# Eight plain row tiles instead of six at the head of a Strassen-Winograd matmul, with a new head order and early casting loads

## The chip, the cores and the metric

The kernel runs on one core of one Trainium2 chip. The metric is the device time of one execution in microseconds (us), taken from several executions; their median is what is compared. A profile of one execution is shown beside it.

## The reference

```python
batch, m, k, n = 16, 512, 1024, 768      # x: (16, 512, 1024), w1 and w2: (1024, 768), all float32
y1 = np.matmul(x, w1)
y2 = np.matmul(x, w2)
return (np.tanh(y1) * y2).astype(np.float32)
```

So there are 8192 rows of x, or 64 row tiles of 128 rows. Each goes through two products, with w1 (t = 0) and with w2 (t = 1), and the two results are joined by a tanh and a multiplication.

## The kernel before

**Two kinds of row tiles.** The first HEAD = 6 row tiles are computed plainly in bfloat16. For one tile and one weight there are 8 steps over the inner dimension (k = 0 to 7), each with a matmul of 512 columns ("F", line 265) and one of 256 columns ("G", line 268). The other 58 row tiles go in 29 pairs. A pair is multiplied by one weight with a Strassen-Winograd scheme in float16: seven block products p1 to p7 (line 399), each of four matmuls of 384 columns, instead of eight. One pair with one weight is a *unit*; there are 58 units. The plain tiles need only a cast of w and a transposed x. The units need more: the power-of-two scale of w (the sum of |w|), the blocks b11, b21, b22 and t1 to t4 of w in float16, a scaled float16 copy of x, its transpose, and the block sums s1 to s4 of the transposed x (line 380).

**Who does what.** TensorE multiplies. The plain tiles 0 to 3 are loaded in float32 and transposed on TensorE (`T00` to `T31`, line 216; `T20` is the first half of the columns of tile 2), and evacuated and cast by `e00` to `e31`. Tiles 4 and 5 are loaded by GpSimd DMAs that cast to bfloat16 (`Lx4`, `Lx5`, line 241) and then transposed by DMA transposes on the queue of SP (`e41`, `e51`, line 245). A one-element GpSimd copy (line 240) from the row block of w2 that has to land first holds each of these casting loads back. The x of the pairs is loaded by SP (`Lp00` is pair 0, upper tile; line 332), summed by ScalarE (`ax`, line 338), scaled by VectorE (`rx`), cast (`cx`, line 358, or on ScalarE line 360) and transposed by a DMA transpose on SP (`Tx00`, `Tx01`, line 366). The weights are loaded as 16 row blocks (`La0` to `La7` for w1, `Lb0` to `Lb7` for w2, line 248), cast (`ca`, `cb`) and summed (`absa`, `absb`, line 258). `parta`, `suma` and `scalea` make the scale of w1 out of the sums; `suma` is a matmul with ones (line 298), into the PSUM bank that SCALE_BANK names. The plain results go through `tanh0F` (ScalarE, line 281) and `mul0F` (VectorE, line 285) and are stored by `st0` to `st5` (line 288). In a unit, ScalarE copies PSUM out (`seed` L413, `s5` and `u2` L417) and does the tanh (L430), and VectorE adds (`c12`, `c22`, L422) and multiplies (L436).

**Order.** Each engine works strictly in its order. For the head and the first ten units (PLANNED = 10) the order on every engine is the list ORDER, written out by hand. A planner walks it (`schedule`) with costs and dependencies only to decide in which order the program emits the instructions. `m41F3` in the lists is tile 4, weight w2, F, k = 3; `p5.0` is product 5 of unit 0. SEQUENCE says which pair and weight a unit is. The remaining units are emitted at slots of a fixed pitch, by a formula. At the head of the SP queue stands LOADS, in which x0 to x3 are loaded in halves, between the blocks of w.

**Rings.** The float32 x has 6 buffers, the 16-bit x (`xh`) 4, the transposed x (`xT`) 10, the output (`o`, one buffer for two tiles) 3. Three PSUM pairs serve the units; the head uses the eight banks as they become free.

Of the kernel before, what the change touches and what calls it, by code (L numbers as in the profile page):

```python
# [13 lines left out]
def kernel(  # L14
# [16 lines left out]
    nc = tc.nc  # L31
# [8 lines left out]
    F = 512  # L40
    G = N - F
    HEAD = 6
# [6 lines left out]
    LOADS = ("x0.0 a0 x1.0 a1 x2.0 a2 x0.1 x3.0 a3 x1.1 x2.1 a4 x3.1 a5 a6 a7 b0 b1 b2 b3 b4 b5 b6 b7").split()  # L49
    ABS = ((1, 1, 1, 1, 1, 1, 1, 1), (2, 0, 2, 0, 2, 0, 1, 1))  # L50
    SCALE_BANK = (3, 1)
# [6 lines left out]
        "e01": "dve", "e10": "act", "e11": "dve", "e20": "act", "e21": "dve", "e31": "dve", "ca0": "act",  # L58
        "ca2": "act", "cx31": "act", "cx40": "act", "cx61": "act"
# [3 lines left out]
            T00 T10 T20 m10F0 m00F0 m20G0 m00G0 T01 T30 m20F0 m00F1 m00F2 T11 m30F0 m30F1 m00F3 m10F1 m10F2  # L63
            T21 m10G0 m00G1 m00G2 m20G1 m10F3 m10F4 m20F1 m20F2 m20F3 m20F4 m20F5 T31 m30F2 m20F6 m00F4 m00F5
            m00F6 m00F7 m20F7 m30G0 m30G1 m30G2 m30G3 m30G4 m30G5 m30G6 m30F3 m30F4 m30F5 m30F6 m30F7 m01G0
            m11F0 m11F1 m11G0 m21G0 m31G0 m31G1 m01F0 m01F1 m11G1 m01G1 m21G1 suma m21G2 m11G2 m11F2 m01G2
            m31G2 m01F2 m00G3 m00G4 m20G2 m20G3 m20G4 m20G5 m20G6 m20G7 m30G7 m00G5 m00G6 m00G7 m10G1 m10G2
            m10G3 m10G4 m10G5 m10G6 m10G7 m10F5 m10F6 m10F7 m31G3 m31G4 m11G3 m11G4 m11G5 m01F3 m01F4 m01F5
            m31G5 m11F3 m01G3 m01G4 m01G5 m40F0 m40F1 m40F2 m40F3 m31G6 m01G6 m11G6 m01G7 m31G7 m40F4 m40F5
            m40F6 m40F7 m11F4 m11F5 m21G3 m21G4 m21G5 m21G6 m21G7 m01F6 m01F7 m11F6 m11F7 m21F0 m21F1 m21F2  # L70
            m21F3 m21F4 m21F5 m21F6 m21F7 m40G0 m50G0 m40G1 m50G1 m50G2 m40G2 m40G3 m40G4 m31F0 m31F1 m31F2
            m31F3 m31F4 m31F5 m31F6 m31F7 m11G7 m50F0 m50F1 m50F2 m50F3 m50F4 m50F5 m50F6 sumb m50F7 m41F0
            m41F1 m41F2 m41F3 m41F4 m40G5 m40G6 m40G7 m50G3 m50G4 m50G5 m50G6 m50G7 m41G0 m51G0 m51G1 m51G2
            m51G3 m51G4 m51G5 m51G6 p1.0 m41G1 m41G2 m41G3 m41G4 m41G5 m41G6 m41G7 p5.0 p2.0 p6.0 m51G7 p3.0
            m41F5 m41F6 m41F7 p7.0 p1.1 p1.2 p4.0 p5.1 p2.1 p6.1 p5.2 p3.1 p7.1 p2.2 p6.2 p4.1 p1.3 p3.2 p7.2
            p5.3 p2.3 p6.3 p4.2 p3.3 p7.3 m51F0 m51F1 m51F2 m51F3 m51F4 m51F5 p4.3 p1.4 p1.5 p5.4 p2.4 p6.4
            p5.5 p2.5 p7.4 p3.4 p6.5 p4.4 m51F6 m51F7 p3.5 p7.5 p1.6 p4.5 p5.6 p2.6 p6.6 p1.7 p3.6 p7.6 p5.7
            p2.7 p4.6 p6.7 p1.8 p5.8 p7.7 p3.7 p2.8 p4.7 p6.8 p1.9 p3.8 p7.8 p5.9 p2.9 p4.8 p6.9 p1.10 p3.9
            p7.9 p5.10 p2.10 p4.9
        """,  # L80
        "act": """
            absa0 e10 ca0 e20 absa1 ca2 absa3 absa2 absa4 absa5 absa6 absa7 tanh0F tanh2F absb0 tanh3F absb2
            b21a b22a tanh2G tanh0G tanh1F ax00 tanh4F absb7 ax01 absb4 absb6 ax10 ax11 tanh5F b11b tanh4G
            seed.0 b22b s5.0 f00.0 u2.0 ax21 b21b seed.1 f10.0 seed.2 s5.1 f00.1 u2.1 f11.0 s5.2 ax20 f11.1
            u2.2 f10.1 f01.0 seed.3 ax31 s5.3 u2.3 ax41 f01.1 ax30 ax40 seed.4 seed.5 s5.4 f00.4 u2.4 cx31
            cx40 s5.5 f01.4 u2.5 f10.4 ax51 seed.6 f11.4 s5.6 f00.6 u2.6 seed.7 ax50 f11.6 f01.6 f10.6 u2.7
            seed.8 s5.7 s5.8 ax60 ax61 u2.8 seed.9 f00.8 cx61 s5.9 f10.8 u2.9 f01.8 f11.8 seed.10 s5.10 f00.10
        """,
        "dve": """
            e00 ca1 e01 e30 ca3 e11 ca4 e21 ca5 ca6 ca7 e31 cb1 cb0 parta cb2 cb4 scalea cb5 cb3 cb6 cb7 b11a  # L90
            t1a t2a t4a t3a mul0F mul1F mul2G rx0 cx00 mul2F cx01 mul3F partb mul0G scaleb sx0 rx1 cx10 sx1
            cx11 s3.0 s1.0 s2.0 s4.0 t1b mul4G c12.0 mul4F c22.0 s3.1 s1.1 s2.1 s4.1 t2b t4b t3b c12.1 c22.1
            f00.2 rx2 cx20 cx21 c12.2 f01.2 c22.2 f11.2 f00.3 f10.2 sx2 c22.3 f11.3 c12.3 f10.3 s1.2 s2.2 rx3
            cx30 rx4 s3.2 s4.2 f01.3 c22.4 c12.4 sx3 cx41 mul5F c12.5 c22.5 s1.3 s3.3 s2.3 s4.3 f00.5 f10.5
            f01.5 f11.5 c12.6 c22.6 rx5 cx50 s1.4 s2.4 s3.4 s4.4 cx51 c22.7 c12.7 f00.7 f01.7 f10.7 sx4 rx6
            cx60 c22.8 s1.5 s2.5 s3.5 c12.8 f00.9 sx5 f11.7 c12.9 c22.9 s4.5 f01.9 f10.9 f11.9
        """,
        "dma": """
            Lx0.0 La0 Lx1.0 La1 Lx2.0 La2 Lx0.1 Lx3.0 La3 Lx1.1 Lx2.1 La4 Lx3.1 La5 La6 La7 Lb0 Lb1 Lb2 Lb3
            Lb4 Lb5 Lb6 Lb7 e41 Lp00 e51 Lp01 Lp10 Lp11 Tx00 Lp20 Tx01 st0 Tx10 Lp21 Tx11 Lp30 st4 st2 st1  # L100
            Lp31 st3 Lp40 Lp41 Tx20 Tx21 store1.2 Lp50 store1.3 Tx30 Lp51 Tx31 store0.3 st5 Tx40 Tx41 store0.2
            Lp60 Lp61 Tx50 Tx51 Tx60 Tx61 store0.7 store1.7 store0.9 store0.5 store1.9 store1.5
        """,
        "pool": """
            Lx4 Lx5
# [19 lines left out]
    smpool = pool("sm", 4)  # L125
# [48 lines left out]
    def op(name, engine, cost, due, needs, fn, *args):  # L174
        plan[name] = (engine, cost, [n for n in needs if n], fn, args)
# [61 lines left out]
    def load_cast_head_x(mt):  # L237
        hb[mt] = xhpool.tile([P, K], bf16, tag="xh", name="x_b")

        pin(nc.gpsimd.tensor_copy(hb[mt][:, :1], w_f[1][:, mt - 2, :1]))  # L240
        pin(nc.gpsimd.dma_start(hb[mt], xf[mt]))
# [162 lines left out]

    SEQUENCE = [(0, 0), (1, 0), (0, 1), (1, 1)] + [(i, t) for i in range(2, PAIRS) for t in range(2)]
# [110 lines left out]

    for n, what in enumerate(LOADS):
        i = int(what[1])
        if what[0] == "x":
            op(f"L{what}", "dma", 0.7, n - 200, [], load_head_x, i, int(what[3]))  # L520
        else:
            op(f"L{what}", "dma", 1.0, n - 200, [], load_w, "ab".index(what[0]), i)
    for mt in range(HEAD):
        if mt < 4:
            for h in range(2):
                op(f"T{mt}{h}", "pe", 0.45, 5 + mt + 4 * h, [f"Lx{mt}.{h}", f"e{mt - 1}{h}" if mt else ""], pe_transpose_f, mt, h)
                op2("e", f"e{mt}{h}", ("dve", "act")[h], 4 + mt + 4 * h, [f"T{mt}{h}", f"e{mt}0" if h else "", f"e{mt - 1}0" if mt and not h else ""],
                   evacuate_f, mt, h)
        else:
            op(f"Lx{mt}", "pool", 2.6, 22, [f"Lb{mt - 2}"], load_cast_head_x, mt)  # L530
            op(f"e{mt}1", "dma", 1.3, 20, [f"Lx{mt}", f"e{mt - 1}0" if mt == 4 else f"e{mt - 1}1"], dma_transpose_head, mt)
    for t in range(2):
        for k in range(KO):
            a = "ab"[t]
            op2("c", f"c{a}{k}", "dve", 6 + 1.3 * k + 12 * t, [f"L{a}{k}"], cast_wb, t, k)
            n = ABS[t][k]
            if n:
                op(f"abs{a}{k}", "act", 0.23 + 0.82 * n, 8 + 1.3 * k + 17 * t, [f"L{a}{k + n - 1}"], abs_w, t, k, n)
# [4 lines left out]
    def accumulate(m, t, which, bank, due):  # L543
# [9 lines left out]
        if t == 0:  # L553
            op(out, "act", 0.62, due(KO), last, head_tanh, banks[bank], m, which == "F")
        else:
            op(out, "dve", 0.68, due(KO) + 3, last + [f"tanh{m}{which}"], head_mul, banks[bank], m, which == "F")
# [24 lines left out]
    if HEAD > 4:  # L581
        for n, (mt, t, which, bank) in enumerate(((4, 0, "F", 3), (5, 0, "F", 5), (4, 0, "G", 7), (4, 1, "F", 6), (4, 1, "G", 3),
                                                  (5, 1, "F", 7))):
            accumulate(mt, t, which, bank, lambda k: 29 + 1.7 * n)
        stores(4)
# [17 lines left out]
    ready = lambda i: 43.5 + 0.65 * 7 * min(position[i, 0], position[i, 1]) - 4  # L603
    x_ring = ["e01", "e11", "e21", "e31"]
    for i in range(FIRST + 1):
        due = ready(i)
        for h in range(2):
            n = 2 * i + h
            x_free = "" if n < 2 else x_ring[n - 2] if n < 6 else f"cx{(n - 6) // 2}{n % 2}"
            h_free = f"Tx{(n - 4) // 2}{n % 2}" if n >= 4 else ""  # L610
            op(f"Lp{i}{h}", "dma", 1.35, due - 12, [x_free, f"Lp{(n - 1) // 2}{(n - 1) % 2}" if n else "Lb7"], load_x, HEAD + n)
# [4 lines left out]
            if n >= 10 - HEAD:  # L616
                r = n - 10 + HEAD
                if r < 4:
                    t_need += [f"m{r}1F7", f"m{r - r % 2}1G7", f"m{r - r % 2 + 1}1G7"]
                elif r < HEAD:  # L620
                    t_need += [f"m{r}1F7", "m41G7", "m51G7"]
                else:
                    t_need += of_unit("p4", (r - HEAD) // 2, 1) + of_unit("p3", (r - HEAD) // 2, 1)
# [16 lines left out]
    for u in range(PLANNED + 1):  # L640
        i, t = SEQUENCE[u]
        for name, (engine, cost, z, needs, fn, args) in unit_ops(u).items():
# [19 lines left out]
            op(f"{name}.{u}", engine, cost, 43.5 + 0.65 * (z + 7 * u), [f"{n}.{u}" for n in needs] + more, fn, *args)  # L662
# [64 lines left out]
```

## Time and profile before

| | us |
|---|---|
| median of 7 runs | 324.84 |
| lowest, highest of them | 322.87, 328.54 |
| the profiled execution, its own time | 328.12 |
| span of that execution (first to last instruction) | 326.3 |
| TensorE busy in the span | 310.7 (95%) |
| VectorE, ScalarE busy | 242.2 (74%), 233.2 (71%) |
| granted TensorE clock, mean | 0.977 |

The profiled execution is one of the longest: it is 3.3 us over the median. What lies outside the span is 328.12 less 326.3, 1.8 us. Busy time of TensorE is not time at its peak, since the matmuls overlap; starts of matmuls are what counts. An engine that is busy 74% of the span can still be late in one place, so the stretches of the head are read one by one.

### The profile page before, as it was taken

The page shows a single profiled execution, that of the slowest core. Times are in us where ns is not written, and L with a number is a line of the kernel's source. Part 1 is how long each engine was busy: PE and PEld are TensorE (multiplying, and loading weights), DVE is VectorE, ACT ScalarE, POOL GpSimd, SP SyncE. Part 2 cuts the span into 40 slices and gives each one's busy share as a digit, 9 for nine tenths or more (in the row PEclk, how much of TensorE's full clock was granted, in tenths as well). Part 3 has the DMA queues.
Part 4 walks back from the last instruction along what each step waited for, and adds up shares of the span by engine and source line. Part 5 has one row for each costly group of instructions (what it writes and reads, how often), then busy time and mean ns, then how long its engine had stood idle before and what let it go on. Part 6 is the DMA issues. An engine that isn't in the chain of part 4 may idle for free.

```text
span 326.3 us, 5430 instructions
## 1 busy us (share of the span) xinstructions
PE 310.7 (95%) x1859; PEld 184.6 (57%) x1859; DVE 242.2 (74%) x565; ACT 233.2 (71%) x454; POOL 7.3 (2%) x15
## 2 busy tenths in 40 slices
PE   5998959999999999999999999999999999999994
PEld 2665534655555555555565555555565555555652
DVE  1468636987878777779877777779877777778642
ACT  4685964888877777777777777777777777776551
POOL 1020000000000000000000000000000000000004
PEclk9699996999999999999999999999999999999999
DMA  6998795978999999999899999998899899985322
GB/s 241 394 398 173 242 176 165 333 215 222 313 257 226 317 282 299 237 283 233 249 242 292 263 279 237 255 278 258 252 215 296 262 272 246 270 250 140 121 96 97
DMA packets 84988, 80.58 MB, mean 247 GB/s; under 512 B 65760, under 2 KB 66272, under 8 KB 84960
## 3 DMA queue, kind: packets, MB, share of 16 engines
q1 hardware_dynamic: 84384, 79.32, 88.0%
q0 software_dynamic: 288, 0.52, 0.9%
q10 hardware_dynamic: 288, 0.39, 0.3%
q8 instruction: 14, 0.23, 0.3%
q14 instruction: 14, 0.11, 0.1%
HBM read 39.85 MB, written 25.17 MB: 199 GB/s over the span
## 4 chain that ended last, share of the span: by engine, by line
PE 81%; DMA 13%; DVE 2%; SPq 2%; issue 0%; POOL 0%; ACT 0%; DVEq 0%
PE bank L399 77%; DMA xT<-x_h 5%; DMA x_f<-in_x_dram 4%; PE bank L265 3%; DMA wf<-in_w_dram 2%; DMA x_b<-in_x_dram 2%; DMA xTb<-x_b 1%; SPq L208 1%; PE bank L268 1%; DVE o L436 1%; SPq L248 1%; DVE s L380 1%; DVE c L422 0%; DVE x_h L358 0%; POOL x_b L240 0%
## 5 line engine op out<-in xcount | busy, mean ns | idle before, releaser
L399 PE MATMUL bank<-t,s 128*128 128x384 f16 x696 | 134.0, 328 | 4.7 <-DVE s L380 4.3
L399 PEld LDWEIGHTS <-s 128*128 128x128 f16 x928 | 91.0, 98 | 67.0 <-DVE s L380 4.9
L399 PEld LDWEIGHTS <-xT 128*128 128x128 f16 x696 | 68.2, 98 | 48.1 <-issue 2.7
L399 PE MATMUL bank<-b,xT 128*128 128x384 f16 x464 | 94.7, 328 | 0.6 <-ACT bank L413 0.6
L338 ACT ACTIVATE junk<-x_f 128x1024 bf16<-128x1024 f32 x58 | 60.8, 1049 | 6.9 <-DMA x_f<-in_x_dram 6.8
L422 DVE TENSOR_TENSOR c<-bank,u 128x384 f32<-128x384 f32 x58 | 32.2, 555 | 44.9 <-PE bank L399 42.3
L430 ACT ACTIVATE th<-c,out_r 128x384 f32<-128x384 f32 x58 | 35.1, 610 | 23.4 <-DVE c L422 23.3
L399 PE MATMUL bank<-b,s 128*128 128x384 f16 x232 | 47.9, 330 | 0.0
L399 PE MATMUL bank<-t,xT 128*128 128x384 f16 x232 | 47.1, 325 | 0.1
L417 ACT ACTIVATE u<-bank 128x384 f32<-128x384 f32 x58 | 28.2, 487 | 19.4 <-PE bank L399 18.8
L358 DVE TENSOR_SCALAR x_h<-x_f,pr 128x1024 f16<-128x1024 f32 x55 | 41.0, 747 | 0.3
L430 ACT ACTIVATE th<-bank,out_r 128x384 f32<-128x384 f32 x58 | 33.3, 574 | 7.0 <-PE bank L399 7.0
L436 DVE SCALAR_TENSOR_TENSOR o<-bank,out_r,th 128x384 f32<-128x384 f32 x58 | 35.4, 611 | 1.8 <-PE bank L399 1.6
L413 ACT ACTIVATE bank<-bank 128x384 f32<-128x384 f32 x58 | 28.0, 482 | 10.7 <-DVE o L436 8.1
L417 ACT ACTIVATE s<-bank 128x384 f32<-128x384 f32 x58 | 27.9, 483 | 10.4 <-PE bank L399 7.9
L422 DVE TENSOR_TENSOR c<-bank,s 128x384 f32<-128x384 f32 x58 | 32.1, 553 | 3.4 <-PE bank L399 1.1
L436 DVE SCALAR_TENSOR_TENSOR o<-c,out_r,th 128x384 f32<-128x384 f32 x56 | 33.7, 606 | 0.1
L380 DVE TENSOR_TENSOR s<-xT 128x512 f16<-128x512 f16 x58 | 23.9, 417 | 5.5 <-DMA xT<-x_h 5.5
L265 PE MATMUL bank<-wb,xTb 128*128 128x512 bf16 x96 | 25.4, 394 | 1.3 <-DMA xTb<-x_b 1.3
L258 ACT ACTIVATE junk<-wf 128x768 bf16<-128x768 f32 (+1 forms) x13 | 12.9, 991 | 4.1 <-DMA wf<-in_w_dram 4.0
L265 PEld LDWEIGHTS <-xTb 128*128 128x128 bf16 x96 | 9.7, 103 | 9.6 <-DMA xTb<-x_b 1.6
L268 PE MATMUL bank<-wb,xTb 128*128 128x256 bf16 x96 | 13.9, 277 | 0.0
(48 smaller groups left out, 140.3 us busy)
## 6 DMA issues: line engine op xcount, KB each, us to landing
x_f<-in_x_dram SPq DMA_DIRECT2D x58, 512.0 KB, 5.8
out_dram<-o SPq DMA_DIRECT2D x62, 384.0 KB, 3.4
wf<-in_w_dram SPq DMA_DIRECT2D x16, 384.0 KB, 7.1
x_f<-in_x_dram SPq DMA_DIRECT2D x8, 256.0 KB, 6.5
xT<-x_h SPq DMA_TRANSPOSE x58, 3.7
x_b<-in_x_dram POOLq DMA_DIRECT2D x2, 256.0 KB, 5.3
out_dram<-o ACTq DMA_DIRECT2D x2, 192.0 KB, 2.0
out_dram<-o SPq DMA_DIRECT2D x2, 192.0 KB, 2.3
```

The costliest lines, as they stand in the source:

```text
L258: pin(nc.scalar.activation(junk[:, :n * N].rearrange("p (k n) -> p k n", n=N), w_f[t][:, k:k + n, :], ACT.Abs, accum_out=asum_w[t][:, j:j ...
L265: pin(nc.tensor.matmul(bank, hx[mt][:, k, :], w_b[t][k][:, :F], start=k == 0, stop=k == KO - 1))
L268: pin(nc.tensor.matmul(bank[:, at_:at_ + G], hx[mt][:, k, :], w_b[t][k][:, F:], start=k == 0 and mt % 2 == 0, stop=k == KO - 1, skip_group ...
L338: pin(nc.scalar.activation(junk[:, :K], xs[HEAD + 2 * i + h], ACT.Abs, scale=2.0 ** -12, accum_out=pair_sum[i][:, h:h + 1]))
L358: pin(nc.vector.tensor_scalar(xh, xs.pop(mt), pair_r[i][:, h:h + 1], None, ALU.mult))
L380: pin((nc.vector if eng == "dve" else nc.gpsimd).tensor_tensor(s, st[i, a], st[i, b], op))
L399: pin(nc.tensor.matmul(bank[:, cols], st[i, a][:, k, :], wt[t][b][:, k, cols], start=start and k == 0, stop=stop and k == KH - 1, skip_gro ...
L413: pin(nc.scalar.activation(ub[u]["b"][:, :Q], ub[u]["a"][:, :Q], ACT.Copy))
L417: pin(nc.scalar.activation(c, ub[u][bank][:, :Q], ACT.Copy))
L422: pin(nc.vector.tensor_tensor(c, ub[u][bank][:, :Q], ub[u][other], ALU.add))
L430: pin(nc.scalar.activation(th, v, ACT.Tanh, scale=rs[i][:, 0, h:h + 1]))
L436: pin(nc.vector.scalar_tensor_tensor(o[:, h, q * Q + cols.start:q * Q + cols.stop], v, rs[i][:, 1, h:h + 1], tanhs[i, h, q][:, cols], ALU. ...
```

## The change

HEAD goes from 6 to 8: tiles 6 and 7 become plain, by the casting load and the DMA transpose that tiles 4 and 5 have, and 28 pairs, 56 units, are left. SEQUENCE takes each pair with w1 and then with w2; before, pairs 0 and 1 went with w1 first, and then both with w2. x0 to x3 are loaded whole. The casting loads of tiles 4 to 7 are held back by row blocks 1, 3, 5 and 7 of w2 (before: 2 and 3 for tiles 4 and 5). Both sums of |w| go into bank 5. The second-stage plain tiles alternate between banks 6 and 7. All orders of the head are written out anew, some casts and evacuations change their engine, a pool of small tiles gets 8 buffers, and the planner counts the casting loads and some other DMA work (this only moves where instructions are emitted).

```diff
-    HEAD = 6
+    HEAD = 8
-    LOADS = ("x0.0 a0 x1.0 a1 x2.0 a2 x0.1 x3.0 a3 x1.1 x2.1 a4 x3.1 a5 a6 a7 b0 b1 b2 b3 b4 b5 b6 b7").split()
+    LOADS = ("x0 a0 x1 a1 x2 a2 x3 a3 a4 a5 a6 a7 b0 b1 b2 b3 b4 b5 b6 b7").split()
-    SCALE_BANK = (3, 1)
+    GATE = {4: 1, 5: 3, 6: 5, 7: 7}
+    SCALE_BANK = (5, 5)
     ELSEWHERE = {
-        "e01": "dve", "e10": "act", "e11": "dve", "e20": "act", "e21": "dve", "e31": "dve", "ca0": "act",
-        "ca2": "act", "cx31": "act", "cx40": "act", "cx61": "act"
+        "e01": "dve", "e11": "dve", "e21": "dve", "e31": "dve", "ca0": "act", "ca1": "act", "ca7": "act",
+        "b22a": "dve", "b22b": "dve", "cx11": "act", "cx40": "act", "cx61": "act"
     }
         "pe": """
...
+            T00 T01 m00F0 m00G0 T10 T11 m10G0 m10F0 m00G1 m00F1 m10G1 m10F1 T20 T21 m20F0 m20G0 m20F1 m20G1
...
+            m01G7 m11F7 m21F7 m21G7 m31G7 m40F0 m40F1 m40F2 m40F3 m40F4 m40F5 m40F6 m40F7 m50F0 m50F1 m50F2
...
+            m50G5 m50G6 m50G7 m41F0 m41F1 m41F2 m40G6 m40G7 m41F3 m41F4 m11G7 sumb m41G0 m51G0 m51G1 m41F5
...
+            m60G4 m60G5 m60G6 m60G7 p1.0 p1.1 p5.0 p6.0 p2.0 p3.0 p2.1 p7.0 m61F0 p5.1 p4.0 p6.1 p3.1 p1.2
...
         "dve": """
...
+            cb5 t1a t2a cb7 mul0F mul1F mul3F mul2F mul2G partb t3a rx0 cx00 cx01 mul0G scaleb sx0 mul4F t4a
+            mul4G mul5F t1b rx1 cx10 s1.0 s2.0 s4.0 s3.0 b22b t2b t3b c22.0 t4b s3.1 s1.1 s2.1 rx2 cx20 c22.1
...
         "dma": """
-            Lb4 Lb5 Lb6 Lb7 e41 Lp00 e51 Lp01 Lp10 Lp11 Tx00 Lp20 Tx01 st0 Tx10 Lp21 Tx11 Lp30 st4 st2 st1
...
+            Lx0 La0 Lx1 La1 Lx2 La2 Lx3 La3 La4 La5 La6 La7 Lb0 Lb1 Lb2 Lb3 Lb4 Lb5 Lx4 Lb6 Lb7 Lx5 e41 Lp00
+            Lx6 e51 Lp01 Lx7 e61 Lp10 e71 Lp11 Tx00 st0 st1 Tx01 Lp20 Tx10 Lp21 Tx11 Lp30 st2 st4 st3 Lp31
...
-    smpool = pool("sm", 4)
+    smpool = pool("sm", 8)
-        pin(nc.gpsimd.tensor_copy(hb[mt][:, :1], w_f[1][:, mt - 2, :1]))
+        pin(nc.gpsimd.tensor_copy(hb[mt][:, :1], w_f[1][:, GATE[mt], :1]))
-    SEQUENCE = [(0, 0), (1, 0), (0, 1), (1, 1)] + [(i, t) for i in range(2, PAIRS) for t in range(2)]
+    SEQUENCE = [(i, t) for i in range(PAIRS) for t in range(2)]
+            if m // 2 >= O_BUFS:
+                last += [f"st{mt}" for mt in range(m // 2 * 2 - 2 * O_BUFS, m // 2 * 2 - 2 * O_BUFS + 2)]
-        for n, (mt, t, which, bank) in enumerate(((4, 0, "F", 3), (5, 0, "F", 5), (4, 0, "G", 7), (4, 1, "F", 6), (4, 1, "G", 3),
-                                                  (5, 1, "F", 7))):
-            accumulate(mt, t, which, bank, lambda k: 29 + 1.7 * n)
-        stores(4)
+    for m in range(4, HEAD, 2):
+        for n, (mt, t, which) in enumerate(((m, 0, "F"), (m + 1, 0, "F"), (m, 0, "G"), (m, 1, "F"), (m, 1, "G"), (m + 1, 1, "F"))):
+            accumulate(mt, t, which, 6 + n % 2, lambda k: 29 + 2.6 * (m - 4) + 1.7 * n)
+        stores(m)
```

In the DMA list the entries Lx4 to Lx7 belong to the GpSimd queue; they stand in one list with SP's for the planner alone.

## The prediction

> **What bounds the kernel now.** The page first: its slices show TensorE full from the third slice on except in slices 4 and 6, and the granted clock low in slices 2 and 7.
>
> ```profile
> PE   5998959999999999999999999999999999999994
> PEclk9699996999999999999999999999999999999999
> ```
>
> So TensorE sets the pace, and what can be won lies in the first 60 us. There I read the timeline of TensorE for the pitch of each kind of matmul. Columns: start, length, what; the pitch is the distance of two starts over the count.
>
> ```profile
> 15.51 0.60 PE L216 MATMUL bank<-ident,x_f 128*128 128x128 f32 x4
> 15.95 0.60 PE L268 MATMUL bank<-wb,xTb 128*128 128x256 bf16 x4
> 16.38 1.67 PE L265 MATMUL bank<-wb,xTb 128*128 128x512 bf16 x7
> 17.89 0.60 PE L216 MATMUL bank<-ident,x_f 128*128 128x128 f32 x4
> ...
> 56.32 1.46 PE L399 MATMUL bank<-b,xT 128*128 128x384 f16 x8
> 57.62 0.81 PE L399 MATMUL bank<-t,xT 128*128 128x384 f16 x4
> ```
>
> A transpose costs 0.11, F 0.216, G 0.109 (4 in 0.43), a matmul of a unit 0.1625. Work before, at full clock: 32 transposes 3.5; 6 tiles x 2 weights x 8 x (0.216 + 0.109) = 31.2; 58 units x 28 x 0.1625 = 263.9; sums 0.3; together 298.9.
>
> Then the chain that ended last, and the same place in the windows (busy us of PE, PEld, DVE, ACT, POOL, then clock, DMA share, GB/s):
>
> ```profile
> 39.16 1.02 PE bank L265 x5
> 40.18 8.56 DMA xT<-x_h
> 48.74 0.02 issue
> 48.76 0.77 DVE s L380 x2
> 49.53 0.05 issue
> 49.58 4.02 PE bank L399 x12
> ```
> ```profile
> 44.00:48.30 4.30, 1.27 (x11) 0.78 (x8) 0.00 (x0) 2.12 (x3) 0.00 (x0) 1.00 1.18 159
> 48.30:55.20 6.90, 5.62 (x18) 2.69 (x19) 4.03 (x6) 2.63 (x6) 0.00 (x0) 0.51 0.67 208
> ```
>
> TensorE runs out of plain work at 45.1 and stands until s1 of pair 0 is there (49.58), because the transpose `Tx01`, issued at 40.18, lands 8.56 us later. Then it runs at half clock until 55.15.
>
> The account of the profiled execution: by 14.2 (end of the first half-clock stretch) TensorE has done 24 transposes, 5 F and 2 G, less a part of the last, 3.7 of the work. The other 295.2 would end at 309.4. Added: 1.5 for `Lx4`/`e41` (TensorE waits 28.9 to 30.4), 4.5 the hole, 5.57 us at half clock 2.8, and 3.7 of small gaps after 55 (0.56 at 94.6, 0.75 at 101.0 and 0.29 at 107.0 are the largest). Sum 321.9; the last matmul ends at 321.75. A tail of 4.55 follows to the end of the span (326.3), and 1.8 lies outside: 328.1. Without the hole the same sum gives 321.0 (320.8 with the measured end), with a hole at full clock 325.4. The median, 324.84, is near the latter and the lowest, 322.87, near a hole of 2: I take it that the hole and its cold stretch make the spread of the runs. So I do not subtract from the median; I build the new time up in the same way.
>
> **Part by part.**
>
> *Eight tiles, 28 pairs.* Work: 8 tiles 41.6, 56 units 254.8, transposes 3.5, sums 0.3, together 300.2: **1.3 more**. It pays only through what it covers.
>
> *x0 to x3 whole.* The stretch to 14.2 is walked through. Bytes landed in before: 0.92 MB at 6.0, 1.31 at 7.8, 1.57 at 8.5, then 0.4 MB a us. The same bytes in the new order give x0 at 4.3, a0 6.0, x1 8.2, a1 9.2, x2 10.5, a2 11.5, x3 12.8, a3 13.8. So T00/T01 at 4.4 to 5.3, m00 from 6.9 (cast on ScalarE 0.83), T10/T11 8.2 to 9.9 at half clock, then four F and four G with k = 0, 1, T20/T21 to 13.6. By 14.2 that is 24 transposes, 4 to 5 F and as many G, 4.1. **0.4 gained**; bounds: 1.7 lost, if the window that released the clock in before is no longer full, and 0.8 gained. I take 0.4, as both walks have TensorE busy through 10.8 to 14.2.
>
> *Casting loads gated earlier.* `Lx4` waits for b1 (19.7) instead of b2 (20.86).
>
> ```profile
> 20.92 0.59 POOL L240 CAST x_b<-wf 128x1 bf16<-128x1 f32 x1 [19.53 <-DMA wf<-in_w_dram]
> 21.82 0.75 POOL L241 DMA_DIRECT2D x_b<-in_x_dram  x1 [0.31 <-POOL x_b L240]
> ```
>
> In this row the load is issued at 21.82, its packets begin at 24.3, and the blocks of w go on landing every 0.97 us up to b7 at 25.7: the load cost w nothing. [...] The wait of 1.5 for x4 goes: m40 now comes behind all of tiles 0 to 3, at 14.2 + (3.5 + 20.8 + 0.3 - 4.1) = 34.7, at the latest 36, and `e41` lands at about 30 (3.15 from issue in the chain). `e51`, `e61`, `e71` come by 34, 37, 40 (a load of 512 KB takes 1.3, a transpose 1.3 behind one), their use is at 37, 45 and 47.
>
> *The hole.* Before `p1.0` stand all of tiles 0 to 5, m60F, m70F, m60G and five G of m70: 3.5 + 31.2 + 4.9 + 0.3. So **p1.0 at 14.2 + 39.9 - 4.1 = 50.0**, with 1 us of handoffs 51.0; `p5.0`, which needs s1.0, two products later at **52.3**. VectorE's list has `mul5F t1b rx1 cx10 s1.0` there. mul5F follows m51F7 (45.0 to 46.0), then 0.68 + 1.81 + 0.6 + 0.75 + 0.42: s1.0 at 49.5 to 50.3. It also needs `Tx01`. On the way to that: `ax01` stands behind tanh4F on ScalarE (37.5), so rx0 is done at 39.5, cx00 and cx01 (0.75 each) at 40.3 and 41.0, Tx00 issued at 40.3. Here is what SP did in before:
>
> ```profile
> 38.22 1.24 SPq L366 DMA_TRANSPOSE xT<-x_h  x1
> 39.56 0.53 SPq L332 DMA_DIRECT2D x_f<-in_x_dram  x1
> 40.18 1.24 SPq L366 DMA_TRANSPOSE xT<-x_h  x1
> 41.51 0.63 SPq L288 DMA_DIRECT2D out_dram<-o  x1
> ```
>
> The new list has st0 and st1 between the two transposes, and st0 waits for mul0G (m11G7 stands just before sumb, 41; so mul0G ends at 42): Tx01 is issued at 43.5. With the 3.5 of the first transpose it lands at 47, with the 8.56 of the second at 52. I take 49: the load of 512 KB that stood ahead of it is gone, two stores of 1.0 are there instead. That is 2.9 before the latest time for s1 (52.3 less 0.42, 51.9), so **the hole closes** (-4.5, and with it -2.8 of half clock). What is late next is VectorE's chain: s1.0 has 2.0 of slack, s2 and s4 (0.42 each) follow in front of p6.0 and p3.0; b22b, t2b, t3b (1.0 each) are used from p6.1 on, 3 to 4 us after they are ready. Here and in the 30s many banks pass from a tanh or mul (0.59, 0.68) to the next tile within some 0.2 us; for these handoffs **+1.0** (0 to 2).
>
> *w1 and w2 in turn, bank 5, smaller pools.* Unit 1 needs b11b at 51.7. scaleb follows sumb (41) behind mul0G, done at 43; b11b and b21b on ScalarE (1.57 each) end at 46.4. Pair 1 is needed 12 products after p1.0 instead of one: that only relaxes. The sum in bank 5 waits for tanh2G, at 23.7, and suma is due at 25. Cost 0.
>
> *DMAs behind.* Two more loads of x and two more transposes by unit 4 are 5.2 of DMA time. In before the 16 engines had nothing in 37.5 to 39 and 53 to 57 (two of the windows' rows read 0.00 and 0.33), about the same. So I leave the 3.7 of small gaps.
>
> The last products, the tail and what is outside are as before. **Sum: 14.2 + (300.2 - 4.1) + 3.7 + 1.0 + 4.55 + 1.8 = 321.3**, 1.1% under the median. About 1% is what a measurement of this kernel can tell from no change, with its spread of 5 us.
>
> **The rivals.**
>
> *The hole closes (0.50).* 321.3, own range 319.5 to 323.5; 0.36 of the 0.50 lies over 1% below the median.
>
> *The hole closes and the feed of the pairs gets looser too (0.10).* Pair 1 is needed 8 us later; the 1.6 of stalls at 94 to 107 and the handoffs vanish: 318.7. Against it: the DMA shares of 1.04 and 1.07 at 80 to 100 in before, and more load here.
>
> *The hole moves (0.12 + 0.20).* Tx01 queues behind four 16-bit transposes and eight x loads since 26 us; if it lands after 51.9, TensorE stands at p5.0, and m61F0 and all units are behind it in the strict order. Up to 3 us late: 322 to 325 (0.12). [...] A hole of 4.5 again, from Tx01 landing after 55: 321.3 + 4.5 + 2.8 = **328.6, slower** (0.20). For it: the 8.56 of before arose in just such a mix of loads, transposes and a store. Against it: 2.9 of slack first.
>
> *The debt is paid later (0.08).* st2, st3 stand behind Tx10, Tx11, Lp21, Lp30; f11.1 on VectorE waits for them at 62. If they land at 64, or Tx20 comes late, 2 to 4 of stalls at 60 to 75: 323.5 to 325.
>
> **Numbers.** Faster by over 1%: 0.36 + 0.10 = 0.46. Within 1%: 0.14 + 0.12 + 0.08 = 0.34. Slower: 0.20. The range 318.0 to 327.8 leaves out most of the cold hole and little below.
>
> **What would show it.** Right: p1.0 starts at 49.5 to 52.5, no TensorE wait over 1 us between 14 and 60, clock 1.0 from 14 on, Tx01 landed before 51.9. Wrong: L399 waiting for DVE s L380 in the fifties, a second half-clock stretch, half clock lasting to 17.6, or `DVE wb L252` waiting over 1 us for wf near 27.

## The result and the profile after

| | median us | lowest to highest | runs |
|---|---|---|---|
| changed kernel | 322.09 | 320.89 to 325.25 | 14 |
| before, beside it | 325.56 | 322.87 to 328.54 | 35 |

The ratio of the times is 0.991, 95% interval 0.9884 to 0.9936 (the two medians alone give 0.989): about 0.9% faster. The median is 0.8 us above the forecast of 321.3. By that ratio the gain lies within the 1% for which the prediction had 0.34, not in its likeliest class, faster by more (0.46). The profiled execution of the changed kernel took 322.65 us with a span of 320.9. The execution of before that is shown ahead of the prediction was a slow one, with a hole of 4.5 us and a half-clock stretch behind it; a second profile of before, of 324.73 us (`b_again` below), stands in for it wherever the two kernels are compared.

The page's slices after, TensorE and its granted clock:

```profile
PE   6999699999989999999999999999999999999993
PEclk9999999999999999999999999999999999999998
```

Slice 6 is full now, and slice 5 (32 to 40 us) has a hole instead. The clock row is lower only at the end. It says nothing of the first 4.8 us: before the first record of the clock the row counts it as full, though the matmuls there run at twice their pitch (those of 512 columns start 0.427 apart, not 0.216). The two windows in which before had its hole and its half clock (busy us of PE, PEld, DVE, ACT, POOL, clock, DMA share, GB/s):

```profile
44.00:48.30 4.30, 4.30 (x22) 2.00 (x21) 3.33 (x4) 4.27 (x7) 0.00 (x0) 1.00 1.10 245
48.30:55.20 6.90, 6.90 (x48) 4.40 (x46) 5.62 (x12) 4.32 (x8) 0.00 (x0) 1.00 0.75 164
```

TensorE is busy in both from end to end. Its timeline through the head, and the only long wait in it:

```profile
31.80 1.89 PE L269 MATMUL bank<-wb,xTb 128*128 128x512 bf16 x8
36.68 1.90 PE L269 MATMUL bank<-wb,xTb 128*128 128x512 bf16 x8 [2.99 <-DMA xTb<-x_b]
...
50.65 1.46 PE L403 MATMUL bank<-b,xT 128*128 128x384 f16 x8
51.95 1.46 PE L403 MATMUL bank<-t,s 128*128 128x384 f16 x8
...
64.70 1.46 PE L403 MATMUL bank<-t,s 128*128 128x384 f16 x8 [0.77 <-DVE c L425]
```

`p1.0` starts at 50.65 and `p5.0` at 51.95, without a wait. The new wait is m50F0 for e51, 33.5 to 36.68. SP's queue where Tx00 and Tx01 are issued, with the two stores between them:

```profile
40.66 1.24 SPq L370 DMA_TRANSPOSE xT<-x_h  x1
42.27 0.85 SPq L292 DMA_DIRECT2D out_dram<-o  x2
43.17 1.94 SPq L370 DMA_TRANSPOSE xT<-x_h  x1
```

Tx01, issued at 43.17, lands at 49.00; VectorE's s1.0 starts at 49.63.

Where the time came from: TensorE's time between the starts of matmuls, less their pitch (0.216, 0.109, 0.1625 and, for the transposes, 0.1075), summed over stretches of the second profile of before and of two of the changed kernel (`a_again`, below, is an execution of 321.07 us, the fastest of its 11):

| stretch, us | before (`b_again`) | changed | changed (`a_again`) |
|---|---|---|---|
| 0 to 14.2 | 5.8 | 3.1 | 3.7 |
| 14.2 to 30 | 1.8 | 0.2 | 0.0 |
| 30 to 45 | 0.9 | 3.4 | 1.7 |
| 45 to 60 | 2.2 | 0.0 | 0.0 |
| 60 to 75 | 0.0 | 0.9 | 0.8 |
| 75 to the end | 4.7 | 3.9 | 3.8 |
| sum | 15.4 | 11.5 | 10.0 |
| work at pitch | 298.6 | 300.0 | 299.9 |

The work grew by 1.3 to 1.4, as counted. The stretch to 14.2 gave 2.1 to 2.7, the wait for x4 1.6 to 1.8, the hole 2.2; 0.8 to 2.5 went back at 30 to 45 and 0.8 to 0.9 at 60 to 75. The 0.8 to 0.9 at the end is no more than executions of one kernel differ there (3.7 in the first profile of before). The net, 2.5 and 4.1, brackets the 3.5 between the medians.

### The profile page after: what moved, and what is told of

It reads as the page before. It is cut to its first block, busy times and chain, and to the rows that moved or that the text cites. A ratio compares the mean times of both kernels' runs of the same rounds, so it can differ in the third digit from the quotient of the medians.

```text
span 320.9 us, 5395 instructions
## 1 busy us (share of the span) xinstructions
PE 307.5 (96%) x1867; PEld 182.7 (57%) x1867; DVE 239.0 (74%) x553; ACT 225.1 (70%) x440; POOL 10.7 (3%) x19
## 4 chain that ended last, share of the span: by engine, by line
PE 80%; DMA 14%; SPq 2%; DVE 1%; issue 1%; ACT 0%; POOL 0%; DVEq 0%
PE bank L403 75%; DMA wf<-in_w_dram 5%; DMA out_dram<-o 4%; PE bank L269 3%; DMA x_b<-in_x_dram 2%; DMA xTb<-x_b 2%; PE bank L272 2%; SPq L336 1%; DVE o L439 1%; SPq L249 0%; SPq L212 0%; DVE c L425 0%; ACT bank L416 0%; SPq L292 0%; SPq L252 0%
## 5 line engine op out<-in xcount | busy, mean ns | idle before, releaser
L403 PE MATMUL bank<-t,s 128*128 128x384 f16 x672 | 127.8, 326 | 0.8 <-DVE c L425 0.8
L403 PEld LDWEIGHTS <-s 128*128 128x128 f16 x896 | 87.4, 98 | 59.8 <-issue 1.4
L403 PEld LDWEIGHTS <-xT 128*128 128x128 f16 x672 | 65.6, 98 | 46.9 <-issue 2.7
L403 PE MATMUL bank<-b,xT 128*128 128x384 f16 x448 | 90.6, 326 | 1.0 <-ACT bank L416 0.5
L342 ACT ACTIVATE junk<-x_f 128x1024 bf16<-128x1024 f32 x56 | 58.7, 1048 | 8.7 <-DMA x_f<-in_x_dram 8.7
L425 DVE TENSOR_TENSOR c<-bank,u 128x384 f32<-128x384 f32 x56 | 30.9, 554 | 43.7 <-PE bank L403 41.2
L403 PE MATMUL bank<-t,xT 128*128 128x384 f16 x224 | 45.2, 325 | 0.6 <-DVE c L425 0.6
L403 PE MATMUL bank<-b,s 128*128 128x384 f16 x224 | 45.6, 326 | 0.0
L269 PE MATMUL bank<-wb,xTb 128*128 128x512 bf16 x128 | 33.7, 379 | 3.7 <-DMA xTb<-x_b 3.0
L433 ACT ACTIVATE th<-bank,out_r 128x384 f32<-128x384 f32 x56 | 32.1, 573 | 4.8 <-PE bank L403 4.8
L425 DVE TENSOR_TENSOR c<-bank,s 128x384 f32<-128x384 f32 x56 | 30.9, 553 | 4.4 <-PE bank L403 3.5
L272 PE MATMUL bank<-wb,xTb 128*128 128x256 bf16 x128 | 21.1, 273 | 0.4 <-DVE xTb L228 0.4
L269 PEld LDWEIGHTS <-xTb 128*128 128x128 bf16 x128 | 12.4, 98 | 14.9 <-DMA xTb<-x_b 3.5
L272 PEld LDWEIGHTS <-xTb 128*128 128x128 bf16 x128 | 12.6, 98 | 6.3 <-DVE xTb L228 0.6
```

Source lines behind the costliest of these rows:

```text
L269: pin(nc.tensor.matmul(bank, hx[mt][:, k, :], w_b[t][k][:, :F], start=k == 0, stop=k == KO - 1))
L272: pin(nc.tensor.matmul(bank[:, at_:at_ + G], hx[mt][:, k, :], w_b[t][k][:, F:], start=k == 0 and mt % 2 == 0, stop=k == KO - 1, skip_group ...
L342: pin(nc.scalar.activation(junk[:, :K], xs[HEAD + 2 * i + h], ACT.Abs, scale=2.0 ** -12, accum_out=pair_sum[i][:, h:h + 1]))
L403: pin(nc.tensor.matmul(bank[:, cols], st[i, a][:, k, :], wt[t][b][:, k, cols], start=start and k == 0, stop=stop and k == KH - 1, skip_gro ...
L425: pin(nc.vector.tensor_tensor(c, ub[u][bank][:, :Q], ub[u][other], ALU.add))
L433: pin(nc.scalar.activation(th, v, ACT.Tanh, scale=rs[i][:, 0, h:h + 1]))
```

## The experiments

Each runs beside before on one chip; a ratio is that of its times to those of before, with its 95% interval. Three of them repeat a kernel unchanged: `b_again` the kernel before, `a_again` the changed kernel, `a_txlate2` the kernel of `a_txlate`.

**A second profile of before (`b_again`).**

> The kernel before once more, for a profile of an execution that is nearer to its median: the one shown is 3.3 us over it. Theory (the hole is in every execution, the two half-clock stretches at 7.4 and 48.3 are not): Tx01 lands over 5 us after its issue and TensorE stands 2 to 4.5 us at p5.0, clock 0.99 or more, span 321.5 to 324. Rival (a usual execution has no hole at all, and the gain of the change is elsewhere): a wait under 1 us at 45 to 50.

One execution, 324.73 us (before beside it 324.74). TensorE's timeline at the start and at the hole:

```profile
11.95 1.49 PE L265 MATMUL bank<-wb,xTb 128*128 128x512 bf16 x3
13.23 0.74 PE L216 MATMUL bank<-ident,x_f 128*128 128x128 f32 x4
...
44.98 0.93 PE L268 MATMUL bank<-wb,xTb 128*128 128x256 bf16 x7
47.91 0.82 PE L399 MATMUL bank<-t,s 128*128 128x384 f16 x4 [2.01 <-DVE s L380]
```

and the chain there:

```profile
41.05 6.02 DMA xT<-x_h
...
47.09 0.77 DVE s L380 x2
```

The hole is there, from the same Tx01, but it is 2.2 us (2.01 idle) and not 4.5, and no half clock follows: four matmuls take 0.65. So an execution at the median loses 2.2 here; the 7.3 (hole and half clock) is of the first profile alone. The half clock of the start, though, is in both: here three F take 1.28 from 11.95, 0.427 each, and the pitch is full only from 13.5 (14.2 in the first profile). The clock row does not show it, as it has no record before 13.5.

**Tx01 ahead of Lp20 in before (`b_swap`).**

```diff
-Tx00 Lp20 Tx01 st0
+Tx00 Tx01 Lp20 st0
```

> The kernel before, with one exchange in the list of SP: Tx01 is issued ahead of Lp20. Theory (the hole of before is the transpose Tx01 queueing behind a load of 512 KB, and the hole with its half-clock stretch is the whole price): Tx01 is issued at 39.6 and lands at 44 to 46, the hole at 45 to 49.6 shrinks to under 1.5, no half clock after it, and the time falls by 3 to 4 us to about 321.5 to 322.5, what the eight tiles reach too. Rival (the transposes are slow because loads and stores are mixed with them at all, or s1 is held by something else): Tx01 lands at 47 or later, the hole stays over 3 us, and the time is within 1 us of before.

323.77 us, ratio 0.9965 (0.9937 to 0.9993). Tx01 is issued at 40.45 and lands at 43.57, and the hole is gone altogether:

```profile
45.01 0.93 PE L268 MATMUL bank<-wb,xTb 128*128 128x256 bf16 x7
45.77 0.81 PE L399 MATMUL bank<-t,s 128*128 128x384 f16 x4
...
52.70 0.82 PE L399 MATMUL bank<-t,s 128*128 128x384 f16 x4 [0.81 <-DVE s L380]
53.95 0.32 PE L399 MATMUL bank<-b,xT 128*128 128x384 f16 x1 [0.43 <-ACT bank L413]
```

The cause of the hole is shown: the load ahead of the transpose. But only 0.7 us came out, not 3 to 4. TensorE, now 2 us earlier, waits 1.6 us at 51.7 to 54: 1.0 for the block sums of pair 1, whose transposes land at 49.07 and 51.78 (49.80 and 51.89 in `b_again`), and 0.6 for a copy of ScalarE's. Closing this hole alone buys little; the feed behind it is nearly as late as before. That part of the theory fell.

**The new head with six tiles (`a_six`).**

```diff
-    HEAD = 8
+    HEAD = 6
```
with all entries of tiles 6 and 7 as plain tiles taken out of the lists.

> The changed kernel with HEAD = 6: everything of tiles 6 and 7 as plain tiles is taken out of its lists, all else (whole x0 to x3, pair order, banks, engines, gates) stays, and 29 pairs are left. Theory (two more plain tiles are the cover, 4.9 us of matmuls ahead of p1.0 and 5.5 among the first units, for 1.3 us of work): TensorE comes to p5.0 at 45 to 47, s1 is there at 47 to 49, so a hole of 2 to 4 us stands there, and the time is 322.5 to 325. Rival (the new loads and order are what gained, the two tiles only cost their 1.3 us): no hole over 1 us, 320 to 321.

327.69 us, ratio 1.0115 (1.0068 to 1.0163): 3.2 above before beside it, where the changed kernel was 3.5 below. TensorE's waits over 0.3 us from 43.5 to 67:

```profile
48.62 1.47 PE L403 MATMUL bank<-t,s 128*128 128x384 f16 x8 [3.24 <-DVE s L384]
55.89 0.81 PE L403 MATMUL bank<-b,s 128*128 128x384 f16 x4 [1.02 <-ACT s L420]
58.79 0.81 PE L403 MATMUL bank<-t,xT 128*128 128x384 f16 x4 [0.67 <-DVE c L425]
59.91 0.81 PE L403 MATMUL bank<-t,s 128*128 128x384 f16 x4 [0.32 <-ACT bank L416]
66.41 0.81 PE L403 MATMUL bank<-b,xT 128*128 128x384 f16 x4 [2.18 <-ACT bank L416]
```

The hole at p5.0 is back (3.24), and 4.2 of waits follow, where the plain matmuls of tiles 6 and 7 stood among the units. Here Tx01 had landed at 46.51; s1.0 started at 48.14, behind VectorE's own t1b and cx10. Of the later waits, ScalarE makes the 1.02 and the 2.18: it had itself stood at an `ax`, for a load of x (2.45 and 1.97), ahead of the copy that TensorE wanted. In this execution the 2.18 was followed by 3.41 us at half clock (from 67.21), 1.7 more. So the two tiles cover the feed of the first units as a whole, the chains of VectorE and ScalarE too. The time is 2.7 above the theory's range: I had counted the hole, and not the waits among the units and the half clock.

**e51 ahead of Lp00 (`a_e51`), and ax00 later with it (`a_e51_act`).**

```diff
-Lx5 e41 Lp00 Lx6 e51 Lp01 Lx7 e61
+Lx5 e41 e51 Lx6 Lp00 Lp01 Lx7 e61
```

> The changed kernel with e51 issued right behind e41, ahead of Lp00. Theory (TensorE's new wait of 3.0 us at 33.5 is e51 queueing behind a 512 KB load and the casting load of tile 7): e51 lands at 32 to 34, the wait falls under 1 us; p5.0 is reached 2 to 3 us earlier and then waits for Tx01 or s1 at about 49.5, so 1.5 to 3 us of the 3 come out: 319 to 320.5. Rival (the wait only moves, all of it, to p5.0, since Tx01 and VectorE's chain end last anyway): within 0.7 us of the changed kernel.

325.64 us, ratio 1.0025 (0.9987 to 1.0063): the whole gain is gone. e51 lands at 33.4 as meant, but the wait is a tile further on. The rows of TensorE and of ScalarE:

```profile
39.29 1.95 PE L272 MATMUL bank<-wb,xTb 128*128 128x256 bf16 x10 [3.12 <-ACT o L285]
```
```profile
35.65 1.06 ACT L342 ACTIVATE junk<-x_f 128x1024 bf16<-128x1024 f32 x1 [7.06 <-DMA x_f<-in_x_dram]
...
36.71 0.58 ACT L285 ACTIVATE o<-bank 128x512 f32<-128x512 f32 x1
37.19 1.47 ACT L262 ACTIVATE junk<-wf 128x1536 bf16<-128x1536 f32 x1
...
38.65 0.59 ACT L285 ACTIVATE o<-bank 128x512 f32<-128x512 f32 x1
```

ScalarE stands 7.06 us at ax00, which needs Lp00; tanh3F, absb4 and tanh4F, which frees the bank that m40G wants, are behind it. From 39.68 TensorE also runs 3.41 us at half clock (the 10 matmuls above take 1.95, at full clock 13 take 1.58). Neither theory had this. It was tested by taking ax00 out of the way:

```diff
-absb2 ax00 tanh3F absb4 tanh4F ax01
+absb2 tanh3F absb4 tanh4F ax00 ax01
```

> The kernel with e51 ahead of Lp00, and on ScalarE ax00 moved behind tanh3F, absb4 and tanh4F. With e51 first alone, e51 landed at 33.4 and its wait went, but TensorE stood 3.3 us at m40G (35.8 to 39.3): ScalarE waited 7.1 us for Lp00 at ax00, with tanh3F, absb4 and tanh4F ready behind it. Theory (head-of-line blocking at ax00 is the whole loss): no TensorE wait over 1 us from 30 to 45; s1 then ends last, as Lp01 and ax01 come 1 to 2 us later, so p5.0 waits 0 to 2 us: 320 to 322. Rival (Lp00 late delays rx0, Tx00 and s1 by as much as the wait saved): a hole of 2 us or more at p5.0, 322.5 to 325.

322.18 us, ratio 0.9938 (0.9907 to 0.997); the 3.12 is gone, no wait from 30 to 45 is over 0.8 idle, and p5.0 (51.41) does not wait. So the order on ScalarE made the loss, 3.5 us between the two medians, the half clock that followed the wait included. But what remains is no better than the changed kernel: m40F now waits 0.74 for e41 (landed 33.20), and later matmuls 0.77 and 0.27 for ScalarE; in all TensorE loses 2.3 at 30 to 45, between the 1.7 and the 3.4 of the changed kernel.

**Later gates (`a_gate`).**

```diff
-    GATE = {4: 1, 5: 3, 6: 5, 7: 7}
+    GATE = {4: 5, 5: 6, 6: 7, 7: 7}
```

> The changed kernel with later gates: the casting loads of tiles 4 to 7 wait for row blocks 5, 6, 7 and 7 of w2. It sizes what the earlier gate costs and brings. In the changed kernel b5, b6, b7 land at 24.2, 25.1, 27.2, in before at 23.8, 24.8, 25.7. Theory (the casting loads share the engines with w, and w has slack while e41 and e51 have none): b7 lands at 25.7 to 26.2, but x4 at 28 to 29, e41 at 32 to 33, e51 at 36 or later, TensorE waits 2 to 5 us in 31 to 37: 323 to 326. Rival (w2 is what holds VectorE and TensorE there): no wait gets longer, and the time falls by up to 1 us.

326.07 us, ratio 1.0016 (0.9992 to 1.0041): 3.0 above the changed kernel beside it (323.11). TensorE:

```profile
34.27 3.56 PE L269 MATMUL bank<-wb,xTb 128*128 128x512 bf16 x8 [2.17 <-DMA xTb<-x_b]
38.63 1.68 PE L269 MATMUL bank<-wb,xTb 128*128 128x512 bf16 x7 [0.80 <-DMA xTb<-x_b]
```

x4 lands at 27.5, hardly later, but e41 only at 34.2 and e51 at 38.6: by their gates the loads of tiles 6 and 7 now run beside the transposes, and I take that as the cause. The 8 F after the first wait take twice their time, in a half-clock stretch of 3.4 us. So the early gates of tiles 5 to 7 pay, against these late ones. Against before's gates nothing is shown, and for tile 4 there is little to gain: x4, issued at 19.3 to 20.5 in the ten profiles with the early gates, landed at 26.3 to 27.5; issued at 21.1 to 21.8 in the three with before's, at 26.9 to 27.2; issued at 23.51 here, at 27.52.

**The slack of Tx01 (`a_txlate`, twice).**

```diff
-Tx00 st0 st1 Tx01 Lp20 Tx10 Lp21 Tx11 Lp30
+Tx00 st0 st1 Lp20 Lp21 Tx01 Tx10 Tx11 Lp30
```

> The changed kernel with Lp20 and Lp21 put ahead of Tx01 on SP. It sizes the slack of Tx01. In the profile of the changed kernel it lands at 49.0 and s1.0 starts at 49.6 behind VectorE's own chain, p5.0 starts at 51.95. Theory: two loads of 1.3 us delay Tx01 to 52 to 54, which is 1 to 3 us behind p5.0, so 0.5 to 3 us are lost (322.5 to 325). Rival (the jam of loads ahead of a transpose costs more than their own time, as 8.56 us in before did): Tx01 lands after 55, a hole of over 3.4 us and a stretch at half clock, 326 or more.

320.74 us in 4 runs, ratio 0.9898 (0.9856 to 0.9941). No loss. Tx01 lands at 50.49, not 52 to 54, and VectorE takes it at once:

```profile
50.52 0.43 DVE L384 TENSOR_TENSOR s<-xT 128x512 f16<-128x512 f16 x1 [1.76 <-DMA xT<-x_h]
```

s1.0 is done at 50.95, p5.0 starts at 51.0 in this execution, so the slack is just used up. In the changed kernel it was 2.5 in both profiles (p5.0 at 51.95 and 50.73, less the 0.42 of s1.0 and the landings at 49.00 and 47.79), where the prediction had 2.9. It was run again:

> The kernel with late Tx01 (Lp20 and Lp21 ahead of Tx01) once more: it was meant to lose and had 320.74 in 4 runs, against 322.1 and 323.1 of the changed kernel in 14 and 11. Theory (the SP queue no longer has Lp21 between Tx10 and Tx11, and Tx01's delay was within the slack): 320.5 to 321.8, ratio to before 0.987 to 0.991. Rival (a draw of few runs): 322 to 323, ratio 0.991 to 0.994, as the changed kernel.

322.14 us in 9 runs, ratio 0.9919 (0.989 to 0.9948). The rival holds: the 320.74 was a draw of few runs. Tx01 lands at 51.42 here, and p5.0 waits 0.2. In both profiles of this kernel the wait of 0.8 to 0.9 at 63 is absent, and that is all that can be said for it.

**The stores earlier (`a_st`, `a_best`).**

```diff
-Tx10 Lp21 Tx11 Lp30 st2 st4 st3 Lp31
+Tx10 st2 st3 Lp21 Tx11 st4 Lp30 Lp31
```

> The changed kernel with st2 and st3 moved ahead of Lp21 on SP, and st4 ahead of Lp30. Theory (the debt: f11.1 on VectorE waits for st3, which stands behind Tx11, Lp21 and Lp30 and lands at 62.3, and TensorE stands 0.9 us at 63.6 for it): st3 lands before 59, no TensorE wait at 63 to 65, 0.5 to 1 us gained, 321 to 321.7. Rival (Tx11 comes 2 us later instead, and s1 of pair 1 takes the place of the store): a wait of 1 us or more before 60, no gain or a loss of up to 1 us.

323.16 us, ratio 0.9938 (0.9907 to 0.9969), against 323.11 of the changed kernel beside it. st3 lands at 54.3 and the wait at 63 is gone, but this one is new:

```profile
58.19 0.81 PE L403 MATMUL bank<-b,s 128*128 128x384 f16 x4 [0.87 <-ACT s L420]
```

The rival holds in its outcome, not in its cause: the wait changes its place, but it is for ScalarE's s5.1, which stood behind ax21 and its load Lp21 (2.30 us, landed 56.03). In `a_best` Lp21 stands behind Lp20, st2 and st3 behind Tx10, st4 behind Tx11:

> The changed kernel with Lp21 behind Lp20 (as in the kernel with late Tx01, but Tx01 stays ahead of both), st2 and st3 behind Tx10, st4 behind Tx11. Theory (what gained in the kernel with late Tx01 was that Lp21 and the stores came out of the way of Tx11 and f11.1; the delay of Tx01 was within its slack): no TensorE wait over 0.5 us from 45 to 85, 320 to 321, at or a little below the kernel with late Tx01 (320.74). Rival (that kernel was only a lucky draw of the early waits, and this stretch is worth nothing): within 0.4 us of the changed kernel beside it.

322.24 us in 6 runs, ratio 0.9907 (0.9873 to 0.9941). The store no longer holds f11.1 (it starts at 61.56, 62.44 in the changed kernel), yet TensorE still waits 0.7 at 63, now for ScalarE:

```profile
61.44 1.06 ACT L342 ACTIVATE junk<-x_f 128x1024 bf16<-128x1024 f32 x1 [1.86 <-DMA x_f<-in_x_dram]
...
63.09 0.47 ACT L416 ACTIVATE bank<-bank 128x384 f32<-128x384 f32 x1
```
```profile
63.62 0.81 PE L403 MATMUL bank<-t,s 128*128 128x384 f16 x4 [0.53 <-ACT bank L416]
```

ScalarE stood 1.86 at ax30 for Lp30, with the copy seed.2 behind it. Inconclusive in time; the debt is the order on ScalarE as much as the store.

**The changed kernel again (`a_again`).**

> The changed kernel once more, as the measure for the three that run beside it, and for how much of its profile is of one execution. In its profile the casting load of tile 4 landed at 27.4 and that of tile 7 at 35.6, in three kernels with the same head at 26.5 and 30.8 to 31.5, and TensorE waited 3.0 us for e51, 0.7 in the kernel with late Tx01. Theory (those waits are the jitter of the transfers of one execution): e51 lands at 34 to 35.5 and the wait is 0.5 to 2 us; 321.5 to 322.5. Rival (the wait is in the order): 3 us again.

323.11 us, ratio 0.9919 (0.9886 to 0.9953). e51 lands at 34.1 here and m50F0 does not wait; the wait is 0.92 idle at m40G, for ScalarE. The 3.0 of the first profile goes with a late casting load of that execution (tile 7's landed at 35.6 there, 30.9 here): in the seven profiles with this order of loads and these gates e51 lands at 34.1 to 34.6 where tile 7's load landed by 31, and at 35.1 to 36.7 where it landed at 32.1 or later. Why that load is late at times is not shown.

**Late Tx01 with ax00 behind tanh3F and absb4 (`a_tx_act`).**

> The kernel with late Tx01, and on ScalarE ax00 moved behind tanh3F and absb4 (it stays ahead of tanh4F). In the changed kernel ScalarE waits 4.5 us for Lp00 at ax00 (33.3) and only then does tanh3F (0.58) and absb4 (1.66), so tanh4F ends at 36.9 and TensorE stands 1 us at m40G. Theory: tanh4F ends 1 to 2 us sooner, the wait of 0.7 to 1.1 at m40G goes, 0.5 to 1.5 us gained over the kernel with late Tx01 beside it. Rival (p5.0 waits for s1 in its place, as Tx01 lands at 50.5 there and s1.0 ends at 50.9): within 0.4 us of it.

321.10 us in 6 runs (320.34 to 321.33), ratio 0.9887 (0.986 to 0.9915); `a_txlate2` beside it 322.14. The point is the best of all, 1.0 under its neighbour. The wait at m40G is absent, though in its profiled execution a wait for e41 (2.14 idle, landed 34.58) came in its place. Its interval overlaps that of the changed kernel: it beats before, and that it beats the changed kernel is likely, not shown.

The order of the pairs by w1 and w2 in turn, and the whole loads of x0 to x3, were not tried alone: the new lists are written around both. Nor were the other banks and the casts that changed their engine. Their share in the gain stays open; without the two tiles (`a_six`, in lists written for eight) they gain nothing together.

## Why the prediction was right

- *The work, +1.3:* measured 1.3 to 1.4.
- *The hole closes:* p1.0 predicted at 51.0, came at 50.65 and 49.43; Tx01 at 49, landed at 49.0 and 47.8; p5.0 did not wait. s1.0 predicted at 49.5 to 50.3 (done), was done at 50.05. The rival of the moved hole needed Tx01 after 51.9. Its two cases part at 3 us late, with no half clock up to there. That was an estimate, and no run shows such a border: waits of 2.2 and 3.1 us were followed by half clock, waits of 3.2 and 2.0 were not (last section).
- *Its size:* wrong as a difference, without effect. The 4.5 + 2.8 of the first profile is 2.2 in an execution at the median, and closing it by exchanging two transfers gave 0.7. The sum held since the new time was built up from work and waits, and not by taking 7.3 off the median.
- *The start, 0.4 gained:* the mis-sized term; it gave 2.1 to 2.7. The changed kernel had done 6.9 and 6.3 us of work by 14.2, not 4.1, with full pitch from 4.8 and 5.2. How much of this is the new order stays open. Both profiles of before are at half clock until 14.2 and 13.5 (3.7 and 4.3 of work), but `b_swap`, with the same head, has full pitch from 5.7 and 5.6 of work; and of the eleven profiles with the new head two (`a_txlate`, `a_best`) fall back to half clock for 3.41 us at 7.7 and 8.2, with 5.5 and 5.1 of work. Nor is it a gain by itself: in `b_swap` TensorE only waited longer for e41 (2.55, not 1.64), and m40 started at 30.34, as in the two profiles of before (30.44, 30.17). With the wait for x4, which goes as forecast since m40 stands behind more work, the stretch up to 30 gave 3.9 to 4.3, against 0.4 and 1.5.
- *Handoffs of 1.0, e51 in good time:* mis-sized the other way, 1.7 to 3.4 at 30 to 45. TensorE came to m50 at 33.5 and 34.0 instead of 36.4, and e51, forecast by 34, landed at 36.6 and 34.1. So the sign "no TensorE wait over 1 us between 14 and 60" failed in the first profile (2.99) and held in the second (0.92). The two errors of about 2 us cancelled. In part they have one root (TensorE earlier by the start); that e51 was late as well is another, and that the sum came within 0.8 is in so far luck.
- *The gate:* in before's row the load cost w nothing, with b7 at 25.7. With the earlier gates b7 landed at 27.24 in one execution and 25.71 in another (before 25.68 and 25.50), so 0.0 to 1.7 later. That alone is no argument against an early gate: with the late gates of `a_gate` e41 landed only at 34.2 and e51 at 38.6, and the time rose by 3.0.
- *The debt later* (0.08) came beside the forecast and not instead of it: 0.8 to 0.9 at 63, in the place named, f11.1 behind st3.

## What to carry to other kernels

A hole at the join of two stages is worth what the feed behind it allows: exchanging two transfers closed it and gave 0.7 us, while the plain matmuls of two more tiles, 4.9 us ahead of the units and 5.5 among the first of them, gave the feed time as a whole. Build a new time from work and waits, and take the waits from an execution near the median. In a strict engine order, an instruction that waits for a load should not stand ahead of ready ones that free a buffer: moving e51 ahead of a load cost 3.5 us through ScalarE's queue, and the waits left in `a_six`, `a_st` and `a_best` have the same form, an `ax` ahead of a copy.

## What the runs showed of the hardware that was not expected

- The clock did not go by the length of one wait: 2.2 us in the kernel with later gates and 3.1 in the one with e51 first were followed by 3.41 us at a granted clock of 0.5, while 3.2 in the six-tile kernel and 2.0 in before's second profile were not. Every stretch in the clock records of before's first profile (3.41, 6.83, 34.13, 6.83, 269.65) and of the changed kernel's (314.03) is a whole number of 3.413 us, the last of each apart. So I take the edges at that distance as windows and estimate, from the starts and pitches of the matmuls, which share of each window TensorE was busy. In before's first profile half clock followed on full clock after windows with a share of 0.28 (3.95 to 7.37) and 0.05 (44.91 to 48.33), and, where the matmuls end, 0.10; no other window at full clock had less than 0.57. In the changed kernel's profile the wait for e51 lies across an edge and leaves shares of 0.41 and 0.66 (32.12 to 38.95), and the clock stayed full; only the last, 0.12 at the end of the matmuls, was followed by half clock. By the same estimate, with the edges counted from where each one's clock changes, the windows were busy for 0.32 with later gates and 0.11 with e51 first, where half clock followed, and for 0.56 and 0.44 in the six-tile kernel, whose wait of 3.2 lies across an edge, and 0.45 in before's second profile, where it did not.
- At half clock, by the same estimate, both stretches of before's first profile that lasted 6.83 have a first window busy for 0.61 and 0.63 (from 7.37 and 48.33), after which the clock stayed at half, and a second one busy throughout (10.78 to 14.19 and 51.74 to 55.15), after which it was full. The window of which the prediction says that it released the clock is that from 10.78 to 14.19.
- A casting load took 4.4 to 7.7 us to land in two profiles of the changed kernel (longest 19.68 to 27.40) and 5.3 to 5.4 in two of before. One and the same load (tile 7's) landed up to 4.7 us apart in two executions, and tile 4's, issued 3.0 to 4.2 us earlier than in the kernel with later gates, landed 0.0 to 1.2 earlier.
